# Six U products behind each head's routing, and 70 experts' activations kept ahead of the V loop instead of 42

## The chip, the core and the metric

The kernel runs on one core of a Trainium2 chip. Time is device microseconds (us) of one execution; lower is better. The kernel before takes 3012.7 us, the median of three runs (3009.31 to 3016.61).

## The reference, cut to what matters

Two transformer blocks on 512 tokens of width 1024. The change lies in the last part, `peer_ffn`: every token picks, in each of 8 heads, 16 experts out of 16384 by a product of two key tables, and adds up `gate * gelu(h . u_e) * v_e` over its 128 experts.

```python
s1 = einsum('bshd,hnd->bshn', q[..., :128], keys1)   # 128 scores for each half of the query
s2 = einsum('bshd,hnd->bshn', q[..., 128:], keys2)
v1, i1 = top_k(s1, 16); v2, i2 = top_k(s2, 16)
vals, c = top_k(v1[..., :, None] + v2[..., None, :], 16)
expert = e1 * 128 + e2                               # e1, e2 taken from i1, i2 at c
act = gelu(einsum('td,ted->te', hb, u_tab[eb]))
out = einsum('te,ted->td', gate * act, v_tab[eb])
```

## The kernel before, in words

All fp32 products are made of three matmuls on halves: `load_w` (line 204 on) loads 128x1024 of a weight, ScalarE writes the high part `wh` (line 194), VectorE the rest `wl` (line 195), and `mm3` (lines 200 to 202) multiplies high by high, low by high and high by low. `wraw`, `wh` and `wl` have three buffers each, shared by every weight of the kernel.

`peer` works in this order. First **routing**, eight heads: the query projection (`proj_tr`, tile `acc`, with `yh` and `yl` as the other side), the key scores (line 1550), copies to `q` and `sc` by ScalarE, and in `route` the searches for the top 16 and the sums that turn places into expert numbers, nearly all of it on VectorE. Then **gates**: for 384 tokens (three of the four tiles of 128) the gate of each token and expert is spread into a table of 128 x 128 values, four tokens to a block, 96 blocks: two VectorE instructions (lines 1525 and 1528), 12 small matmuls (1533), one ScalarE copy (1535), and a store to the DRAM table `Gd` for each 16 tokens (1538).

For these 384 tokens all 16384 experts are computed, 128 at a time. `up(e)` makes the **U product** of group e: 24 matmuls of 384 columns into tile `A`, then Gelu into `w`. The **V loop** takes e from 0 to 127: it fetches a piece of the gate table (`g`, eight experts ahead), multiplies `w` by it (line 1471), splits the result into halves, and adds the **V product**, 18 matmuls of 512 columns, to six PSUM banks (`acc`). Two banks are left for `A`.

The first `AHEAD` = 42 U products stand ahead of the V loop. 30 of their results stay in the 31 buffers of `w`; 12 (`SPILL`, every third from 6 to 39) go to DRAM through `wd`, with two buffers `ws`, and are read back in the loop. In an iteration whose e isn't in `SPILL`, the loop makes the next U product.

The last 128 tokens are done by **gathers**, 128 of them, spread over the loop by the table `pace`. One gather (line 1412, GpSimd) reads 128 rows of 8 KB from `uv` by index into `r` (three buffers); VectorE multiplies and adds up (1415), ScalarE does Gelu and the gate (1417, 1418), VectorE adds the result to `x` (1419), which frees the buffer. An iteration's gathers are released by a small ScalarE copy of their indices, `eg` (1486). `pace` gives 9 to an iteration with a U product, 4 to one without that isn't spilled, 0 to a spilled one.

The order on each engine is set by a scheduler when the program is built; the engines then run their instructions strictly in that order.

Of the kernel before, what the change touches and what calls it, by code (L numbers as in the profile page):

```python
# [7 lines left out]
F32 = mybir.dt.float32  # L8
# [4 lines left out]
AF = mybir.ActivationFunctionType  # L13
# [8 lines left out]
LOWP, GDN_AHEAD, SB_AHEAD, U_AHEAD = 1500, 1500, 200, 3000  # L22
# [9 lines left out]

ROT = ((("p", "gd", "p", "sz"), ("g", "gd")), (("p",), ("g",)))

UP = 30
SPILL = range(6, 42, 3)
AHEAD = UP + len(SPILL)


CAND = ((0, 1, 16), (1, 3, 8), (4, 4, 4), (8, 8, 1))  # L40
# [142 lines left out]
class Prog:  # L183
# [664 lines left out]
    def gdn(s, one, two, Y):  # L848
# [14 lines left out]
        for k in range(8):  # L863
            s.mm3(b[:16, :], (wbh[:, 16 * k:16 * k + 16], wbl[:, 16 * k:16 * k + 16]), (Y[0][:, k, :], Y[1][:, k, :]),
                  k == 0, k == 7)
        bf = two.tile([128, NT, 128], F32, name="U", tag="U", bufs=1).rearrange("p t d -> p (t d)")[:16, :]
        nc.vector.tensor_copy(bf, b[:16, :])
# [67 lines left out]
        def head(h):  # L935
# [39 lines left out]

            U, T = BT("U", 1), BT("T", 1)

# [3 lines left out]
            def half(x, m, j):  # L981
                return x.rearrange("p t (b j c) -> p t b j c", j=2, c=m)[:, :, :, j, :]
# [8 lines left out]
            def mh(l, r, m, j, g):  # L991

                r = half(r, m, j)
                o = bank()[:, :128]
                for u, i in enumerate(range(*g)):
                    nc.tensor.matmul(o[:, 64 * u:64 * u + 64], lhsT=l[:, i, :], rhs=r[:, i], start=True, stop=True)
                return o.rearrange("p (t b c) -> p t b c", t=2, c=m)
# [4 lines left out]
            def mm(l, r, g):  # L1002
                o = bank()
                for u, i in enumerate(range(*g)):
                    x = o[:, 128 * u:128 * u + 128]
                    if r is None:
                        nc.tensor.transpose(x, l[:, i, :], s.ident)
                    else:
                        nc.tensor.matmul(x, lhsT=l[:, i, :], rhs=r[:, i, :], start=True, stop=True)
                return o.rearrange("p (t d) -> p t d", t=2)  # L1010
            p1 = part(1)
            for g in pairs:
                w = slice(*g)
                nc.gpsimd.tensor_tensor(U[:, w], s.ident[:, None, :].to_broadcast([128, 2, 128]), p1[:, w], ALU.subtract)
                nc.scalar.activation(T[:, w], mm(U, None, g), AF.Copy)
            for m in LEV:
# [5 lines left out]
                for g in pairs:  # L1022
                    w = slice(*g)
                    u_ = half(U, m, 1)[:, w]
                    nc.vector.tensor_tensor(u_, u_, mh(y, U, m, 1, g), ALU.subtract)
                for g in pairs:
                    w = slice(*g)
                    nc.scalar.activation(half(T, m, 0)[:, w], half(mm(U, None, g), m, 0), AF.Copy)
            A, B = slice(0, 64), slice(64, 128)
            y = two.tile([128, NT, 64], F32, name="y", tag="y", bufs=1)  # L1030
            for g in pairs:
                w = slice(*g)
                o = bank()[:, :128].rearrange("p (t d) -> p t d", t=2)
                for u, i in enumerate(range(*g)):
                    nc.tensor.matmul(o[B, u, :], lhsT=N[A, i, B], rhs=T[A, i, A], start=True, stop=True)
                nc.scalar.activation(y[B, w], o[B], AF.Copy)
            for g in pairs:
                w = slice(*g)
                o = bank()[:, 128:].rearrange("p (t d) -> p t d", t=2)
                for u, i in enumerate(range(*g)):  # L1040
                    nc.tensor.matmul(o[A, u, :], lhsT=y[B, i, :], rhs=U[B, i, B], start=True, stop=True)
                nc.scalar.activation(U[A, w, B], o[A], AF.Copy, scale=-1.0)
            vc, kc = BT("vc", 1), BT("kc", 1)
# [184 lines left out]
    def stick(s, ctx, Y):  # L1228
# [15 lines left out]
        def head(h):  # L1244
# [9 lines left out]
            for js in ((3, 2), (1,), (0,)):  # L1254
# [29 lines left out]
                nc.vector.tensor_tensor(e, e, x[:, :w], ALU.add)  # L1284
                A = two.tile([128, 512], F32, name="A", tag="t1", bufs=1)[:, :w]
                nc.scalar.activation(A, e, AF.Exp)
                for j in js:
# [66 lines left out]
    def peer(s, Y):  # L1354

        nc, tc, a = s.nc, s.tc, s.a
        ND = 128 * DT
        NG = ND // TG
        with ExitStack() as ctx:
            P = lambda name, bufs, **k: ctx.enter_context(tc.tile_pool(reuse_waits="tile", name=name, bufs=bufs, **k))  # L1360
            one, two, gp = P("p_one", 1), P("p_two", 2), P("p_g", 2)
# [7 lines left out]

            s.E = one.tile([128, NT, 2, 128], F32, name="E")  # L1370
            s.gate = one.tile([128, NT, 8, 16], F32, name="gate")
            with tc.tile_pool(reuse_waits="tile", name="p_rt", bufs=2) as rt:
                s.rank = rt.tile([128, 16, 16 * NT], BF, name="rank", bufs=1)
                nc.scalar.activation(s.rank, s.iota[:, :16, None].to_broadcast([128, 16, 16 * NT]), AF.Copy)
                for h in range(8):
                    q = {}

                    def ev(f, b, q=q):
                        q[f] = rt.tile([128, 512], F32, name="q", tag=f"q{f}")
                        nc.scalar.activation(q[f], b, AF.Copy)  # L1380
                    s.proj_tr(Y, a["w_pq"][h], ev, tag="acc", first=h == 0)
                    s.route(rt, q, keys, h)

                g = s.gate.rearrange("p i h r -> p (i h) r")
                n = 8 * NT
                sm = rt.tile([128, n], F32, name="sm")
                nc.vector.tensor_copy(sm, g[:, :, 0])
                nc.vector.tensor_tensor(g, g, sm[:, :, None].to_broadcast([128, n, 16]), ALU.subtract)
                nc.scalar.activation(g, g, AF.Exp)
                nc.vector.tensor_reduce(sm, g, AX.X, ALU.add)  # L1390
                nc.vector.reciprocal(sm, sm)
                nc.vector.tensor_tensor(g, g, sm[:, :, None].to_broadcast([128, n, 16]), ALU.mult)
# [25 lines left out]
                nc.scalar.activation(wt[:, c], wt[:, c], AF.Copy, scale=gx[:, c])  # L1418
                nc.vector.scalar_tensor_tensor(x, r[:, 1024:], wt[:, c], x, op0=ALU.mult, op1=ALU.add)  # L1419
            acc = None  # L1420
            wd = s.dram.tile([len(SPILL), 128, ND], F32, name="wd")

            def up(e):
                with tc.high_priority(offset=U_AHEAD) if e < 6 else nullcontext():
                    U = s.load_w(a["ut"][e], 1024)
                A = s.bank("A")[:, :ND]
                for k in range(8):
                    s.mm3(A, U(128 * k, 128), (Y[0][:, k, :ND], Y[1][:, k, :ND]), k == 0, k == 7)
                if e in SPILL:
                    w = two.tile([128, ND], F32, name="ws", bufs=2)  # L1430
                else:
                    w = two.tile([128, ND], F32, name="w", bufs=UP + 1)
                    wq[e] = w
                nc.scalar.activation(w, A, AF.Gelu)
                if e in SPILL:
                    nc.sync.dma_start(wd[SPILL.index(e)], w)
            wq = {}
            ahead = AHEAD
            for e in range(ahead):
                up(e)  # L1440

            room, n = [0], ahead
            for e in range(128):
                both = e not in SPILL and n < 128
                room.append(room[-1] + (9 if both else 0 if e in SPILL else 4))
# [13 lines left out]
            for e in range(128):  # L1459
                if e not in SPILL and ahead < 128:  # L1460
                    up(ahead)
                    ahead += 1
                if e in SPILL:
                    wq[e] = two.tile([128, ND], F32, name="ws", bufs=2)
                    nc.sync.dma_start(wq[e], wd[SPILL.index(e)])
                if e + 8 < 128:
                    fetch(e + 8)
                w = wq[e]
                w3 = w.rearrange("p (g t) -> p g t", t=TG)
                with tc.issue_after(subs[e - 2].ins) if e > 1 else nullcontext():  # L1470
                    nc.vector.tensor_tensor(w3, w3, gs[e // 8][:, :, e % 8, :], ALU.mult)
                wh = two.tile([128, ND], F32R, name="wh")
                wl = two.tile([128, ND], F32R, name="wl")
                last = s.split(wh, wl, w)
                subs.append(s.sub)
                V = s.load_w(a["uv"][128 * e:128 * e + 128, 1024:], 1024)
                if acc is None:
                    acc = [[s.bank("acc") for n in range(2)] for i in range(DT)]
                for i in range(DT):
                    for n in range(2):  # L1480
                        t = slice(128 * i, 128 * i + 128)
                        s.mm3(acc[i][n], (wh[:, t], wl[:, t]), V(512 * n, 512), e == 0, e == 127)
                js = slice(pace[e], pace[e + 1])
                if js.stop > js.start:
                    with tc.issue_after(last.ins):
                        nc.scalar.activation(eg[:, js], ei[:, js], AF.Copy)  # L1486
                for j in range(js.start, js.stop):
                    gather(j)
# [139 lines left out]
```

## Time and profile before

| | us |
|---|---|
| median of three runs | 3012.7 (3009.31 to 3016.61) |
| the profiled execution | 3021.56 |
| its span | 3019.8 |

| engine | busy us | share of the span |
|---|---|---|
| TensorE matmul (PE) | 2901.3 | 96% |
| TensorE weight load (PEld) | 2602.8 | 86% |
| VectorE (DVE) | 2012.7 | 67% |
| ScalarE (ACT) | 1340.5 | 44% |
| GpSimd (POOL) | 607.4 | 20% |

Busy shares are means over the whole span; matmuls overlap in the trace, so a stretch in which PE is busy all the time can still have few matmuls in it, and their number in a stretch says more. DMA moved 549.62 MB, 182 GB/s over the span; in its last third 277 to 350 GB/s in most stretches of 50 us.

### The profile page before, as it was taken

How to read it: one execution, taken by the hardware profiler on the slowest of the kernel's cores; microseconds unless marked ns; L12 is line 12 of the kernel's file. 1: busy time of each engine (PE TensorE's matmuls, PEld its weight loads, DVE VectorE, ACT ScalarE, POOL GpSimd, SP SyncE). 2: the span in 40 equal slices, each digit the busy share in tenths (PEclk: the TensorE clock that was granted, in tenths of full speed). 3: DMA queues.
4: the chain of work that ended last, by engine and by line, in shares of the span. 5: the costliest groups of instructions: out<-in, count | busy, mean ns of one | idle time of the engine just before them, and what ended most of it. 6: DMA issues, size and time to landing. Idle time of an engine off the chain costs nothing. (4 is left out here: it accounts for less than half of the span.)

```text
span 3019.8 us, 44411 instructions
## 1 busy us (share of the span) xinstructions
PE 2901.3 (96%) x17102; PEld 2602.8 (86%) x17103; DVE 2012.7 (67%) x3633; ACT 1340.5 (44%) x2383; POOL 607.4 (20%) x587
## 2 busy tenths in 40 slices
PE   8999999999899999999999799997999999999998
PEld 7877878888789999999988599997888889988977
DVE  5986445553566676765345997775667788787875
ACT  5244433332455565656423345554334344444432
POOL 3001010000455555452200000000111222222210
PEclk9999999999999999999999899998999999999999
DMA  5321132223345555454763134445788899988985
GB/s 194 98 71 63 57 98 98 97 92 98 109 143 161 150 159 161 137 168 141 228 228 127 53 107 143 169 175 180 244 301 307 297 323 337 334 328 299 332 279 198
DMA packets 200149, 549.62 MB, mean 182 GB/s; under 512 B 17360, under 2 KB 90704, under 8 KB 179072
## 3 DMA queue, kind: packets, MB, share of 16 engines
q1 hardware_dynamic: 149184, 358.34, 36.0%
q0 software_dynamic: 49600, 184.76, 17.5%
q10 hardware_dynamic: 1152, 3.67, 0.4%
q8 instruction: 134, 2.20, 0.3%
q14 instruction: 79, 0.65, 0.1%
HBM read 476.52 MB, written 70.19 MB: 181 GB/s over the span
## 5 line engine op out<-in xcount | busy, mean ns | idle before, releaser
L195 DVE TENSOR_TENSOR wl<-wraw,wh 128x1024 fp32r<-128x1024 f32 x474 | 590.3, 1246 | 305.3 <-ACT wh L194 303.4
L194 ACT ACTIVATE wh<-wraw 128x1024 fp32r<-128x1024 f32 (+1 forms) x495 | 520.8, 1054 | 581.6 <-PE bank L201 126.7
L1412 POOL DMA_INDIRECT r<-in_uv_dram,eg x128 | 175.6, 1372 | 1162.7 <-ACT eg L1486 945.9
L202 PE MATMUL A<-yh,wl 128*128 128x384 f32 x1024 | 346.3, 338 | 7.5 <-DVE wl L195 7.4
L200 PE MATMUL A<-yh,wh 128*128 128x384 f32 x1024 | 345.6, 338 | 3.9 <-ACT wh L194 3.3
L201 PE MATMUL A<-yl,wh 128*128 128x384 f32 x1024 | 344.6, 336 | 0.0
L200 PE MATMUL acc<-wh 128*128 128x512 f32 x768 | 304.1, 399 | 19.4 <-ACT wh L194 19.4
L201 PE MATMUL acc<-wl,wh 128*128 128x512 f32 x768 | 305.5, 398 | 0.9 <-DVE wl L195 0.9
L202 PE MATMUL acc<-wh,wl 128*128 128x512 f32 x768 | 292.6, 397 | 3.8 <-DVE wl L195 3.8
L1415 DVE SCALAR_TENSOR_TENSOR r<-r,hx 128x1024 f32<-128x1024 f32 x128 | 156.3, 1221 | 110.1 <-DMA r<-in_uv_dram,eg 108.7
L200 PE MATMUL p<-yh,wh 128*128 128x256 f32 x736 | 214.1, 291 | 7.0 <-DVE l L195 3.8
L202 PE MATMUL p<-yh,wl 128*128 128x256 f32 x736 | 215.7, 293 | 1.4 <-DVE wl L195 1.4
L201 PE MATMUL p<-yl,wh 128*128 128x256 f32 x736 | 213.4, 290 | 0.0
L202 PEld LDWEIGHTS A<-yh,wl 128*128 128x128 f32 x1024 | 192.9, 188 | 10.6 <-DVE wl L195 10.5
L200 PEld LDWEIGHTS A<-yh,wh 128*128 128x128 f32 x1024 | 193.2, 189 | 8.5 <-ACT wh L194 4.2
L201 PEld LDWEIGHTS A<-yl,wh 128*128 128x128 f32 x1024 | 193.1, 189 | 3.7
L200 PEld LDWEIGHTS acc<-wh 128*128 128x128 f32 x768 | 146.2, 190 | 51.0 <-ACT wh L194 20.8
L201 PE MATMUL bank<-yl,wh 128*128 128x512 f32 (+1 forms) x480 | 184.1, 384 | 0.3 <-DMA yl<-od 0.3
L202 PE MATMUL bank<-yh,wl 128*128 128x512 f32 (+1 forms) x480 | 183.5, 383 | 0.0
L200 PE MATMUL bank<-yh,wh 128*128 128x512 f32 (+1 forms) x480 | 182.8, 383 | 0.1
L202 PEld LDWEIGHTS acc<-wh,wl 128*128 128x128 f32 x768 | 145.2, 189 | 39.0 <-DVE wl L195 5.1
L201 PEld LDWEIGHTS acc<-wl,wh 128*128 128x128 f32 x768 | 146.4, 191 | 33.6 <-DVE wl L195 3.2
(576 smaller groups left out, 6914.8 us busy)
## 6 DMA issues: line engine op xcount, KB each, us to landing
wraw<-in_ut_dram SPq DMA_DIRECT2D x128, 512.0 KB, 4.7
wraw<-in_uv_dram SPq DMA_DIRECT2D x128, 512.0 KB, 6.2
Gd<-g SPq DMA_DIRECT2D x24, 1024.0 KB, 4.4
g<-Gd SPq DMA_DIRECT2D x128, 192.0 KB, 7.6
wraw<-in_w_up_dram SPq DMA_DIRECT2D x44, 512.0 KB, 3.7
wraw<-in_w_sb_dram SPq DMA_DIRECT2D x24, 512.0 KB, 4.3
wraw<-in_w_down_dram SPq DMA_DIRECT2D x22, 512.0 KB, 3.8
wraw<-in_w_out_dram SPq DMA_DIRECT2D x16, 512.0 KB, 3.8
```

What stands on the lines that cost most here:

```text
L194: r = nc.scalar.activation(h, src, AF.Copy)
L195: s.sub = (nc.gpsimd if eng == "pool" else nc.vector).tensor_tensor(l, src, h.bitcast(F32), ALU.subtract)
L200: nc.tensor.matmul(out, lhsT=L[0], rhs=R[0], start=start, stop=False)
L201: nc.tensor.matmul(out, lhsT=L[0], rhs=R[1], start=False, stop=False)
L202: nc.tensor.matmul(out, lhsT=L[1], rhs=R[0], start=False, stop=stop)
L1412: nc.gpsimd.indirect_dma_start(out=r, out_offset=None, in_=a["uv"], in_offset=bass.IndirectOffsetOnAxis(ap=eg[:, j:j + 1], axis=0))
L1415: nc.vector.scalar_tensor_tensor(r[:, :1024], r[:, :1024], 1.0, hx, op0=ALU.mult, op1=ALU.mult, accum_out=act[:, c])
```

## The change

`up`, `wq` and the DRAM tile `wd` are defined ahead of routing, and after each head's `route` six U products follow in the program: 48 of them by the end of routing. `AHEAD` becomes 70, and the other 22 follow after the gates as before. 30 results stay in `w`; the other 40 go through DRAM. `pace` isn't edited, but is worked out from `SPILL` and `AHEAD`, so that it gives nothing to 40 iterations instead of 12 and more to the rest. The V loop makes 58 U products instead of 86.

```diff
-UP = 30
-SPILL = range(6, 42, 3)
-AHEAD = UP + len(SPILL)
+
+AHEAD, UP, UPS = 70, 30, 6
+SPILL = [e for e in range(AHEAD) if e > 1 and e not in {AHEAD * k // (UP - 1) for k in range(UP - 1)}]
...
                     s.proj_tr(Y, a["w_pq"][h], ev, tag="acc", first=h == 0)
                     s.route(rt, q, keys, h)
+                    for e in range(UPS * h, UPS * h + UPS):
+                        up(e)
...
             ahead = AHEAD
-            for e in range(ahead):
+            for e in range(8 * UPS, ahead):
                 up(e)
```

The definition of `up` moves up unchanged, from below the gathers to above the routing:

```python
            def up(e):
                with tc.high_priority(offset=U_AHEAD) if e < 6 else nullcontext():
                    U = s.load_w(a["ut"][e], 1024)
                A = s.bank("A")[:, :ND]
                for k in range(8):
                    s.mm3(A, U(128 * k, 128), (Y[0][:, k, :ND], Y[1][:, k, :ND]), k == 0, k == 7)
                if e in SPILL:
                    w = two.tile([128, ND], F32, name="ws", bufs=2)
                else:
                    w = two.tile([128, ND], F32, name="w", bufs=UP + 1)
                    wq[e] = w
                nc.scalar.activation(w, A, AF.Gelu)
                if e in SPILL:
                    nc.sync.dma_start(wd[SPILL.index(e)], w)
```

The scheduler puts the instructions in another order. Two places show it. The first is ScalarE in routing, from the copies of the scores (`sc`) of one head on; `wh` is the high half of a weight, `q` a projection, `xr` the found places, `w` and `ws` Gelu of a U product. Before (fourth and fifth head):

```order
L1552 ACTIVATE sc<-acc 128x512 x2
L1380 ACTIVATE q<-acc 128x512
L1569 ACTIVATE xr<-ix 128x1024 x2
L194 ACTIVATE wh<-wraw 128x1024
L1380 ACTIVATE q<-acc 128x512
L1552 ACTIVATE sc<-acc 128x512 x2
L194 ACTIVATE wh<-wraw 128x1024
L1380 ACTIVATE q<-acc 128x512
```

Now (sixth head):

```order
L1554 ACTIVATE sc<-acc 128x512 x2
L194 ACTIVATE wh<-wraw 128x1024
L1385 ACTIVATE w<-A 128x384
L194 ACTIVATE wh<-wraw 128x1024
L1385 ACTIVATE ws<-A 128x384
L1571 ACTIVATE xr<-ix 128x1024
L194 ACTIVATE wh<-wraw 128x1024
L1571 ACTIVATE xr<-ix 128x1024
L1385 ACTIVATE w<-A 128x384
L194 ACTIVATE wh<-wraw 128x1024
L1385 ACTIVATE ws<-A 128x384
L194 ACTIVATE wh<-wraw 128x1024
```

Between one head's scores and the next there stood only projections; now six U products stand there, each with its split and its Gelu.

The second place is VectorE at the end of the V loop. `wl<-wraw` is the low half of a V weight, `wl<-w` that of the activations, `w<-w,g` the product with the gates; `r` and `x` belong to the gathers. The last instructions before:

```order
L1471 TENSOR_TENSOR w<-w,g 128x384
L195 TENSOR_TENSOR wl<-wraw,wh 128x1024
L195 TENSOR_TENSOR wl<-w,wh 128x384
L195 TENSOR_TENSOR wl<-wraw,wh 128x1024
L195 TENSOR_TENSOR wl<-w,wh 128x384
L1495 TENSOR_TENSOR r<-r,acc 128x512 x6
```

Now, around the last split; behind the last row here follow six more pairs like the last two rows, and a seventh with the six sums into the output between its two instructions:

```order
L1438 SCALAR_TENSOR_TENSOR x<-r,wt,x 128x1024
L1434 SCALAR_TENSOR_TENSOR r,act<-r,hx 128x1024
L195 TENSOR_TENSOR wl<-w,wh 128x384
L1438 SCALAR_TENSOR_TENSOR x<-r,wt,x 128x1024
L1434 SCALAR_TENSOR_TENSOR r,act<-r,hx 128x1024 x2
L1438 SCALAR_TENSOR_TENSOR x<-r,wt,x 128x1024 x2
L1434 SCALAR_TENSOR_TENSOR r,act<-r,hx 128x1024
L1438 SCALAR_TENSOR_TENSOR x<-r,wt,x 128x1024
```

The last gather stood 8 iterations ahead of the end; now 10 first and 11 second gather instructions stand behind the last split that a V product needs. In all, 45 U products stand ahead of the first V product on TensorE before, and 73 now (the loop's first U products are let in while buffers are free); and of the 96 blocks of gates the last 23 now have no U product beside them, where 8 had none.

## Rows read from the trace of the kernel before

**Rows 1.** Tile acc: count, min/median/max ns, first and last start (us).
```profile
L1533 PE MATMUL acc<-p,ehot x1152: 284/297/303, 1850.0 to 2087.4; 128*128 128x128 bf16 x192
L200 PE MATMUL acc<-wh x768: 387/392/795, 2104.5 to 3013.7; 128*128 128x512 f32 x192
L200 PE MATMUL acc<-yh,wh x144: 278/389/628, 1626.2 to 1754.8; 128*128 128x512 f32 x112, 128*128 128x256 f32 x32
```

**Rows 2.** Timeline of TensorE in the V loop: start, duration, instruction.
```profile
2859.77 0.34 PE L200 MATMUL A<-yh,wh 128*128 128x384 f32 x1
...
2863.96 0.39 PE L200 MATMUL acc<-wh 128*128 128x512 f32 x1
...
2868.14 0.34 PE L200 MATMUL A<-yh,wh 128*128 128x384 f32 x1
```

**Rows 3.** Busy us (instructions) of PE, PEld, DVE, ACT, POOL in routing; then granted clock.
```profile
1700.00:1725.00 25.00, 12.70 (x61) 10.22 (x59) 25.00 (x172) 4.40 (x6) 0.00 (x0) 0.84 0.04 15
1725.00:1750.00 25.00, 19.37 (x85) 16.11 (x85) 25.00 (x140) 6.55 (x8) 0.00 (x0) 0.80 0.23 71
...
1650.00:1825.00 175.00, 150.22 (x771) 135.79 (x771) 174.43 (x990) 68.68 (x89) 0.00 (x0) 0.92 0.28 86
```

**Rows 4.** Timeline of ScalarE in routing: the scores of three heads.
```profile
1712.19 1.22 ACT L1552 ACTIVATE sc<-acc 128x512 f32<-128x512 f32 x2 [1.07 <-issue]
...
1751.52 1.06 ACT L1552 ACTIVATE sc<-acc 128x512 f32<-128x512 f32 x2
...
1762.93 1.08 ACT L1552 ACTIVATE sc<-acc 128x512 f32<-128x512 f32 x2
```

**Rows 5.** Waits of TensorE, 1640 to 1850 us: total, times, longest.
```profile
PE acc L202 <- DVE wl L195: 17.9, 1, 17.9
```

**Rows 6.** VectorE's splits from 1650 to 1825 us, by line: busy, mean ns, idle before.
```profile
L195 DVE TENSOR_TENSOR wl<-wraw,wh 128x1024 fp32r<-128x1024 f32 x27 | 32.5, 1217 | 0.1
```

**Rows 7.** Timeline of the last gate blocks: eight without a U product beside them.
```profile
2073.13 3.56 DVE L1528 TENSOR_TENSOR p<-ehot,T 128x1536 bf16<-128x1536 bf16 x4
...
2076.15 11.50 PE L1533 MATMUL acc<-p,ehot 128*128 128x128 bf16 x96
...
2080.61 0.69 DVE L1525 TENSOR_TENSOR ehot<-iota,T 128x1024 bf16<-128x1024 bf16 x1 [0.41 <-PE acc L1533]
```

**Rows 8.** Waits of TensorE from 2104 to 2300 us.
```profile
PE acc L200 <- ACT wh L194: 16.8, 1, 16.8
```

**Rows 9.** The same view in the V loop; last columns: clock, DMA share, GB/s.
```profile
2872.00:3014.00 142.00, 134.89 (x560) 106.73 (x560) 97.82 (x134) 49.83 (x99) 17.59 (x12) 0.98 0.68 236
2450.00:2800.00 350.00, 346.47 (x1734) 312.41 (x1733) 277.98 (x345) 147.79 (x325) 82.56 (x60) 1.00 0.90 324
```

**Rows 10.** DMA issues: count, KB each, median us from issue to landing.
```profile
wraw<-in_uv_dram SPq DMA_DIRECT2D x128, 512.0 KB, 6.2
g<-Gd SPq DMA_DIRECT2D x128, 192.0 KB, 7.6
...
wd<-ws SPq DMA_DIRECT2D x12, 192.0 KB, 1.9
```

**Rows 11.** Timeline of one gather: issue, first and second VectorE instruction.
```profile
2920.27 1.80 POOL L1412 DMA_INDIRECT r<-in_uv_dram,eg  x1 [10.79 <-DVE wl L195]
...
2928.93 1.23 DVE L1415 SCALAR_TENSOR_TENSOR r<-r,hx 128x1024 f32<-128x1024 f32 x1 [1.18 <-DMA r<-in_uv_dram,eg]
...
2932.15 1.28 DVE L1419 SCALAR_TENSOR_TENSOR x<-r,wt,x 128x1024 f32<-128x1024 f32 x1
```

**Rows 12.** VectorE's gather instructions in the loop, by line: busy, mean ns, idle before.
```profile
L1419 DVE SCALAR_TENSOR_TENSOR x<-r,wt,x 128x1024 f32<-128x1024 f32 x128 | 163.7, 1279 | 12.8 <-ACT wt L1418 12.8
L1415 DVE SCALAR_TENSOR_TENSOR r<-r,hx 128x1024 f32<-128x1024 f32 x128 | 156.3, 1221 | 110.1 <-DMA r<-in_uv_dram,eg 108.7 <-DMA g<-Gd 0.9
```

**Rows 13.** Waits from 2130 to 2990 us: GpSimd.
```profile
POOL r L1412 <- ACT eg L1486: 945.9, 70, 505.9
```

**Rows 14.** Timeline of the end: the last split of activations, and the stores.
```profile
3006.63 0.56 DVE L195 TENSOR_TENSOR wl<-w,wh 128x384 fp32r<-128x384 f32 x1 [2.00 <-ACT wh L194]
3013.38 2.72 SPq L1498 DMA_DIRECT2D out_dram<-r  x3
```

More of the change, by code (lines that the diff above doesn't have):

```diff
@@ L1371, in peer, with up @@
             s.gate = one.tile([128, NT, 8, 16], F32, name="gate")
+            wd = s.dram.tile([len(SPILL), 128, ND], F32, name="wd")
+            def up(e):
+                with tc.high_priority(offset=U_AHEAD) if e < 6 else nullcontext():
+                    U = s.load_w(a["ut"][e], 1024)
+                A = s.bank("A")[:, :ND]
+                for k in range(8):
+                    s.mm3(A, U(128 * k, 128), (Y[0][:, k, :ND], Y[1][:, k, :ND]), k == 0, k == 7)
+                if e in SPILL:
+                    w = two.tile([128, ND], F32, name="ws", bufs=2)
+                else:
+                    w = two.tile([128, ND], F32, name="w", bufs=UP + 1)
+                    wq[e] = w
+                nc.scalar.activation(w, A, AF.Gelu)
+                if e in SPILL:
+                    nc.sync.dma_start(wd[SPILL.index(e)], w)
+            wq = {}
             with tc.tile_pool(reuse_waits="tile", name="p_rt", bufs=2) as rt:
@@ L1420, in peer @@
             acc = None
[L1421 to L1437, printed above, removed]
             ahead = AHEAD
-            for e in range(ahead):
+            for e in range(8 * UPS, ahead):
                 up(e)
```

## The prediction

> **What bounds the kernel now.** I read the stages first, from the first and last start of the matmuls into `acc` [rows 1]: routing's projections from 1626.2 us, gates from 1850.0 to 2087.4, V products from 2104.5 to 3013.7. The reader is to see three stretches: 224 us of routing with the first U products, 238 us of gates, and 909 us of V loop.
>
> Then the timeline of TensorE in the loop [rows 2]: a U product starts at 2859.77, the next V product at 2863.96, the next U product at 2868.14. So a U product costs 4.19 us and a V product 4.18 us of TensorE, back to back. The order gives 45 U products ahead of the loop, hence 83 + 128 = 211 products in it: 882 us of its 909. The loop is TensorE-bound, with some 27 us lost. In it VectorE is busy 277.98 of 350 us, and DMA moves 324 GB/s at a share of 0.90 [rows 9]: both are second bounds not far away.
>
> Last the stretches of routing [rows 3]: VectorE is busy all the time, TensorE issues 61 and 85 matmuls in 25 us at a granted clock of 0.84 and 0.80. One pair of heads shows the hole: the scores of one head come at 1712.19, of the next at 1751.52, and then at 1762.93 [rows 4], 39.3 us against 11.4. TensorE waits 17.9 us there for one weight split [rows 5], which in VectorE's order stands behind the routing of two heads; the slow clock does the rest.
>
> **The change part by part.**
>
> *Products moved.* 73 instead of 45 U products stand ahead of the loop: 28 x 4.19 = 117 us more there, 117 less in the loop. Net 0: moving work on a full engine gains nothing, only filled holes do.
>
> *The hole in routing.* With U products behind each head it should close: 39.3 - 11.4 = **-28**. A head then costs TensorE 11.4 + 6 x 4.19 = 36.5 us. VectorE needs for it (174.4 - 32.5) / 8 = 18 us of routing [rows 3, 6], as nearly all eight heads lie in that stretch, and 8 splits of 1.22 us (six U, two projection): 28 us. So VectorE keeps up. Its order has three splits ahead of each head's searches and the fourth behind 27 short instructions, about 6 us, while three products feed TensorE for 12.5. ScalarE, busy 68.7 of 175 us [rows 3], has room for 48 splits and Gelus. For handovers at the projection's end I add **+4** (0 to +10). The gain's ends: -34, if slack at the other heads goes too, and -5, if splits still wait behind routing.
>
> *Gates.* The last 23 blocks instead of 8 have no U product beside them. Eight take TensorE 11.5 us, 1.44 each; VectorE needs 3.56 / 4 + 0.69 = 1.58 a block [rows 7]. 15 x 0.14 = **+2**. The wait for the gate table through DRAM, 16.8 us [rows 8], stays: no U product is left for it, as before.
>
> *Spills.* 28 more stores and reads of 192 KB on SP's queue. Each store waits there for its Gelu, with the next weight loads behind it; but three weight buffers are 12.5 us of products, a load lands in 6.2 and such a store in 1.9 [rows 10]. **0**; without that cover at most 28 x 1.9 = +53, which I exclude, since a store's wait ends with its own product.
>
> *The loop, denser.* The 128 gathers and 128 V weights must now pass in fewer products. In VectorE's order 47 gathers stand from e = 72 to 104, beside 32 V and 28 U products: 60 loads of 0.524 MB, 32 gate pieces of 0.197, 47 gathers of 1.05 make 87 MB in 60 x 4.18 = 251 us, 347 GB/s. From 104 to 128 it is 36 MB in 100 us. DMA has held 324 GB/s for 350 us at a share of 0.90 [rows 9]; in proportion a full share is 360. So it just fits: **+6**, between 0 and, if 324 were the limit, 123 MB / 324 = 379 us instead of 351, +28. VectorE fits too: 47 x (1.22 + 1.28) + 60 x 1.22 + 64 x 0.55 = 226 of 251 us [rows 6, 12, 14]. The 27 us lost elsewhere in the loop I leave; they could shrink by some 15.
>
> *The end.* This is the term that decides. Before, the gathers ran on ScalarE's release, not on buffers: GpSimd waited 945.9 us for `eg` [rows 13], and the last gather lay 8 iterations ahead of the end. Now `pace` gives nothing to 40 iterations, so the gathers start late and then come at the pace of their three buffers; in VectorE's fixed order 10 first and 11 second instructions stand behind the last split. Nothing can put them earlier. Lower end: 10 x 1.22 + 11 x 1.28 = 26.3 us [rows 12], and 7 for sums and store, against 3019.8 - 3006.6 = 13.2 from the last split to the end now [rows 14]: +20. Upper end: at the cycle of a buffer inside the loop, issue at 2920.27, second instruction done at 2933.4 [rows 11], 13.2 / 3 = 4.4 a gather: 44 + 7 - 13 = +38. With the weight loads gone the 8.7 us from issue to landing must shorten, so I take the middle, 3.4 a gather: **+28**.
>
> What a lone gather would take is not in this trace. The Trainium skill's page "DMA: Bandwidth & Descriptors" (Anatomy of one DMA — SWDGE (gpsimd) path) gives a fit of 2.0 us plus bytes over 436 GB/s, an estimate of 4.4 us for 1.05 MB, half of the 8.7 seen under load. By it a buffer's cycle would be 4.4 + 4.5 = 8.9 us, 3.0 a gather, the end +24 instead of +28 and the sum lower by 4.
>
> **Sum:** -28 + 4 + 2 + 0 + 6 + 28 = **+12 us**. The profiled execution took 3021.56 (span 3019.8 and 1.8 around it), 8.9 above the median of 3012.7; it becomes 3034, and the median **3025**.
>
> **Rivals.**
> *Faster.* The loop sheds its own waits: with 55 U products in it instead of 83, fewer loads share the three weight buffers, and of the 27 us lost 14 go; the gathers at the end run at VectorE's floor and DMA costs nothing: -28 + 2 + 20 - 14 = -20, **2993**. It decides once the loop's losses fall below some 20 us with the end at its floor. Against it: 12 of the 27 are lost in the last 142 us, which hold 31 V products worth 130 and hardly a U product [rows 9], and there the gathers now get denser.
> *No change.* End at the floor, DMA free: -28 + 4 + 2 + 20 = -2, **3011**.
> *DMA-bound.* The dense part runs at 324 GB/s and late gathers stop VectorE, as 108.7 us of waits for them do already [rows 12]; the end runs at 4.4 a gather: -28 + 4 + 2 + 28 + 38 = +44, **3057**.
> *The change doesn't do what it says.* TensorE still waits for splits in routing, -5 instead of -28: +35, **3048**.
>
> **How the numbers follow.** About 0.2% (6 us) is what a measurement can tell from no change. Forecast, +6 to +25: 0.35. DMA-bound: 0.22. Routing not filled: 0.10. No change: 0.15. Faster: 0.18. So faster 0.18, same 0.15, slower 0.67. The range, 2996 to 3056, leaves out the outer halves of the faster and of the DMA-bound case, 0.2 in all. The slower cases alone reach from 3019 to 3060.
>
> **What would show it.** Right: no stretch of routing with under 100 matmuls in 25 us; first V product 117 - 28 + 4 + 2 = 95 us later, near 2200; last V product 909 - 117 + 6 = 798 us behind it, near 2998; then 20 to 40 us in which only VectorE, ScalarE and gathers work, with GpSimd waiting for `x` instead of `eg`. Wrong: holes left in routing; a loop with far fewer than 250 matmuls in 50 us; or gathers that are done when the last V product ends. If the loop lasts under 780 us on TensorE, the faster rival is true; if over 815, the DMA-bound one.

## The result, and the profile after

The changed kernel takes 3038.7 us (median of five runs, 3028.9 to 3043.5), the kernel before 3009.9 beside it (3008.6 to 3016.6): a ratio of 1.0081, 95% interval 1.0060 to 1.0102, so 18 to 31 us slower. The forecast was slower, 3025 with a range of 2996 to 3056. The profiled execution took 3038.29 us with a span of 3036.5.

In the code of the changed kernel the gather stands in line 1431, VectorE's two instructions for it in 1434 and 1438, the copy `eg` in 1488, the gate matmuls in 1535. First tile `acc` again, with the columns of [rows 1]:

```profile
L1535 PE MATMUL acc<-p,ehot x1152: 285/298/303, 1949.9 to 2169.6; 128*128 128x128 bf16 x192
...
L200 PE MATMUL acc<-wh x768: 388/393/793, 2184.5 to 2993.4; 128*128 128x512 f32 x192
...
L202 PE MATMUL acc<-wh,wl x768: 387/393/628, 2189.4 to 2995.0; 128*128 128x512 f32 x192
L200 PE MATMUL acc<-yh,wh x144: 283/389/562, 1623.3 to 1899.4; 128*128 128x512 f32 x112, 128*128 128x256 f32 x32
```

The first V product starts at 2184.5 instead of 2104.5, and the V loop lasts 810.5 us instead of 909.7. Against [rows 1] the span divides like this:

| | before | after | products moved | what is left |
|---|---|---|---|---|
| first V product at | 2104.5 | 2184.5 | 28 x 4.19 = +117 | -37 |
| V loop (first to last start of its V matmuls) | 909.7 | 810.5 | -117 | +18 |
| last V product to the span's end | 5.6 | 41.5 | | +36 |
| span | 3019.8 | 3036.5 | | +17 |

The last matmul of the loop stands on line 202, before at 3014.2, after at 2995.0. The two profiled executions differ by 17 us, the medians by 29. The profiled run of before lay 9 to 12 us above its medians, that of after at its own, so 12 us of the difference are in no trace: no run shows in which stretch a faster execution of before saves them.

Routing and the loop by windows; columns as in [rows 3], the last two being the DMA share and GB/s:

```profile
1700.00:1725.00 25.00, 25.00 (x138) 23.24 (x137) 16.15 (x65) 8.50 (x12) 0.00 (x0) 1.00 0.39 122
1725.00:1750.00 25.00, 25.00 (x131) 23.07 (x130) 19.73 (x87) 10.18 (x13) 0.00 (x0) 1.00 0.48 142
1650.00:1825.00 175.00, 175.00 (x958) 165.35 (x957) 135.35 (x618) 68.67 (x93) 0.00 (x0) 1.00 0.43 133
...
2300.00:2750.00 450.00, 430.31 (x2017) 370.23 (x2016) 337.60 (x430) 176.74 (x371) 106.31 (x66) 0.99 0.89 312
2750.00:2900.00 150.00, 150.00 (x725) 131.74 (x724) 123.78 (x158) 63.22 (x144) 37.02 (x26) 1.00 0.93 335
2900.00:3000.00 100.00, 88.35 (x364) 69.71 (x362) 86.05 (x114) 38.68 (x87) 30.68 (x19) 0.95 0.84 299
3000.00:3036.00 36.00, 0.00 (x0) 0.00 (x0) 20.97 (x27) 3.49 (x14) 6.93 (x5) 0.50 0.80 293
```

The hole in routing is gone: TensorE is busy 175.00 of 175 us with 958 matmuls at a granted clock of 1.00 (the 2.4 GHz level), against 150.22, 771 and 0.92, a mixture of the two levels, before [rows 3]. From 2300 to 2750 the loop has become thin: 430.31 of 450 us and 2017 matmuls, where the kernel before had, in the same window,

```profile
2300.00:2750.00 450.00, 446.81 (x2228) 401.63 (x2226) 353.49 (x440) 189.36 (x414) 102.62 (x75) 1.00 0.90 324
```

Part of the smaller number is the mix: a V product has 18 matmuls, a U product 24, and both take about 4.2 us. In the last 36 us TensorE does nothing at all.

TensorE's only wait from 1640 to 2200 us worth naming, in the list of waits (total, times, longest), stands where that of [rows 8] stood:

```profile
PE acc L200 <- ACT wh L194: 14.6, 1, 14.6
```

Who waits in the loop, in the same list from 2200 to 2960 us:

```profile
POOL r L1431 <- ACT eg L1488: 897.9, 28, 596.2
POOL r L1431 <- DVE x L1438: 245.2, 58, 13.2
...
ACT wh L194 <- PE acc L201: 102.0, 60, 3.5
DVE r L1434 <- DMA r<-in_uv_dram,eg: 97.8, 44, 8.9
```

GpSimd now also waits for buffers (`x`, 245.2 us), and VectorE 97.8 us for gathers that haven't landed; in the kernel before that was 93.8 us in the same window. The timeline of the end, from the last split of activations:

```profile
2987.48 0.55 DVE L195 TENSOR_TENSOR wl<-w,wh 128x384 fp32r<-128x384 f32 x1
...
2989.37 1.22 DVE L1434 SCALAR_TENSOR_TENSOR r<-r,hx 128x1024 f32<-128x1024 f32 x1
...
2995.62 1.94 POOL L1431 DMA_INDIRECT r<-in_uv_dram,eg  x1 [4.22 <-DVE x L1438]
...
3002.28 1.23 DVE L1434 SCALAR_TENSOR_TENSOR r<-r,hx 128x1024 f32<-128x1024 f32 x1 [2.50 <-DMA r<-in_uv_dram,eg]
...
3021.86 1.23 DVE L1434 SCALAR_TENSOR_TENSOR r<-r,hx 128x1024 f32<-128x1024 f32 x1 [0.77 <-DMA r<-in_uv_dram,eg]
...
3024.97 1.28 DVE L1438 SCALAR_TENSOR_TENSOR x<-r,wt,x 128x1024 f32<-128x1024 f32 x1
...
3026.27 0.32 SPq L1494 DMA_DIRECT2D r<-x  x1
...
3031.06 1.28 DVE L1497 TENSOR_TENSOR r<-r,acc 128x512 f32<-128x512 f32 x2 [3.62 <-DMA r<-x]
```

Ten gathers are used behind that split, from 2989.37 to 3021.86: nine steps of 3.61 us. The last ends at 3026.25, and 10.2 us of sums and stores follow: the sums' inputs `r<-x` use the gathers' buffers, so the last of them is loaded only at 3026.27, and VectorE waits 3.62 us for it.

### The profile page after: what moved, and what is told of

It reads as the page before. It is cut to its first block, busy times and chain, and to the rows that moved or that the text cites. A ratio compares the mean times of both kernels' runs of the same rounds, so it can differ in the third digit from the quotient of the medians.

```text
span 3036.5 us, 44530 instructions
## 1 busy us (share of the span) xinstructions
PE 2899.4 (95%) x17103; PEld 2599.8 (86%) x17103; DVE 2018.9 (66%) x3633; ACT 1341.6 (44%) x2364; POOL 631.7 (21%) x587
## 4 chain that ended last, share of the span: by engine, by line
PE 68%; DMA 10%; issue 10%; DVE 7%; POOL 3%; ACT 2%; SPq 0%; DVEq 0%; POOLq 0%; ACTq 0%
PE bank L201 6%; PE bank L200 6%; PE bank L202 6%; DMA r<-in_uv_dram,eg 5%; PE A L202 4%; PE A L200 4%; PE A L201 4%; PE acc L1535 4%; PE p L200 4%; PE p L201 3%; PE p L202 3%; PE acc L201 3%; PE acc L200 3%; PE acc L202 3%; PE gd L996 2%
## 5 line engine op out<-in xcount | busy, mean ns | idle before, releaser
L1431 POOL DMA_INDIRECT r<-in_uv_dram,eg x128 | 198.8, 1553 | 1197.6 <-ACT eg L1488 897.9
L200 PE MATMUL acc<-wh 128*128 128x512 f32 x768 | 280.0, 400 | 22.4 <-ACT wh L194 22.4
L202 PE MATMUL acc<-wh,wl 128*128 128x512 f32 x768 | 286.1, 397 | 0.5 <-DVE wl L195 0.5
```

The lines of the kernel that those rows point to most:

```text
L200: nc.tensor.matmul(out, lhsT=L[0], rhs=R[0], start=start, stop=False)
L202: nc.tensor.matmul(out, lhsT=L[1], rhs=R[0], start=False, stop=stop)
L1431: nc.gpsimd.indirect_dma_start(out=r, out_offset=None, in_=a["uv"], in_offset=bass.IndirectOffsetOnAxis(ap=eg[:, j:j + 1], axis=0))
```

## The experiments

**What is the filled hole worth alone?** Two kernels go back to 42 experts ahead, 12 of them through DRAM, and keep products behind each head: five in one, as shown, and three (`42, 30, 3`) in the other.

```diff
-AHEAD, UP, UPS = 70, 30, 6
-SPILL = [e for e in range(AHEAD) if ...]
+AHEAD, UP, UPS = 42, 30, 5
+SPILL = range(6, 42, 3)
```

Five: 

> The V loop, the spills and the pace as in the kernel before (42 ahead, 12 through DRAM), but 40 of the 42 U products behind the heads' routing, five each, so that none is left for the gates. Theory: the hole in routing closes (about -37 us, as in the changed kernel's first V product), but the 96 gate blocks run without U products at VectorE's 1.58 us instead of TensorE's 1.37, which gives back 96 x 0.2 = 20 us: about 3010 - 17 = 2993. Rival (gates alone run at TensorE's pace): about 3010 - 37 = 2973.

Three: 

> The V loop, the spills and the pace as in the kernel before, 24 of the 42 U products behind the heads' routing, three each, 18 left for the gates. Theory: the hole in routing closes and the gates keep enough U products to stay on TensorE, the loop and its end are those of before: first V product near 2104 - 35 = 2069, time about 3010 - 35 = 2975 us. Rival (the gain of the changed kernel ahead of the loop came from having more U products there, not from filling the hole): less than 10 us faster than before, above 3000.

Measured: 2985.8 us, ratio to before 0.9895 [0.9868, 0.9922], and 2983.4 us, 0.9893 [0.9873, 0.9913]. Tile `acc` of the kernel with three, and one window of its gates:

```profile
L1535 PE MATMUL acc<-p,ehot x1152: 282/297/302, 1865.2 to 2056.6; 128*128 128x128 bf16 x192
L200 PE MATMUL acc<-wh x768: 387/392/792, 2072.2 to 2984.5; 128*128 128x512 f32 x192
```
```profile
2000.00:2050.00 50.00, 49.79 (x413) 46.22 (x414) 50.00 (x69) 37.47 (x35) 0.00 (x0) 1.00 0.46 190
```

As many products stand ahead of the loop as before, and the first V product comes 32.3 us earlier; the loop lasts 912.7 us as against 909.6. The filled hole is worth 32 us, and 24 products fill it as well as 40 or 48. With three behind each head the theory came out; with five the time lies between the theory's 2993 and the rival's 2973. The rest of the change, from 42 to 70 experts ahead, costs 3038.7 - 2983.4 = 55 us, or 60 with each kernel taken against the kernel before that ran beside it. The window shows that gate blocks without a U product pass at 413 / 12 = 34.4 in 50 us, 1.45 us each, with VectorE and TensorE both full.

**More experts ahead, the hole left as it was.**

```diff
-AHEAD, UP, UPS = 70, 30, 6
+AHEAD, UP, UPS = 70, 30, 0
```

> UPS from 6 to 0 in the changed kernel: 70 activations ahead of the V loop as before, but all behind routing, none behind a head. Theory (the gain of the change is the filled hole alone, about 37 us, and everything else in it is loss): the first V product comes at 2104.5 + 25 x 4.19 = about 2209 us, the loop and the end stay as in the changed kernel (some 815 + 41), so the span ends near 3066, 30 us or more behind the changed kernel. Rival (the U products between the heads cost VectorE and ScalarE elsewhere what they fill): the first V product at about 2185 to 2195 and a span like the changed kernel's, 3036.

Measured: two runs, 3044.5 and 3064.1 us, ratio 1.0130 [1.0085, 1.0175]. The interval overlaps that of the changed kernel, so it isn't shown to be slower than that, and the spans of the profiled executions differ by only 6 us (3042.7 and 3036.5). The first V product starts at 2190.8, 18 us ahead of the theory's 2209, in the range that the rival had named, but not for its reason: routing has its hole as before, and what is gone is the wait of [rows 8]. TensorE's waits from 1640 to 2200 us:

```profile
PE acc L202 <- DVE wl L195: 17.9, 1, 17.9
...
PE acc L1552 <- ACT q L1397: 4.0, 1, 4.0
```
```profile
2093.00:2191.00 98.00, 98.00 (x567) 97.97 (x566) 30.63 (x28) 35.34 (x51) 0.00 (x0) 1.00 0.62 199
```

The window between the last gate block and the first V product is full of U products: they ran while the gate table came back through DRAM. Products put behind routing's heads fill one hole and are no longer there for the other. Both holes need only a few, as the next kernel shows.

**Four products held back for the second hole.** On the kernel with three products behind each head, the 42nd to the 45th U product are kept on TensorE behind the last gate matmul (`s.glast`).

```diff
-            def up(e):
+            def up(e, after=None):
...
-                for k in range(8):
-                    s.mm3(A, U(128 * k, 128), ...)
+                with tc.issue_after(after) if after else nullcontext():
+                    for k in range(8):
+                        s.mm3(A, U(128 * k, 128), ...)
...
-                up(e)
+                up(e, s.glast.ins if e >= ahead - 1 else None)
...
-                    up(ahead)
+                    up(ahead, s.glast.ins if ahead < AHEAD + 3 else None)
```

> The kernel with 42 activations ahead and three products behind each head, with four U products (the 42nd to the 45th) held on TensorE behind the last gate block, so that they run while the gate table comes back from DRAM. In that kernel TensorE waited 15.3 us for the first V product there, and with none behind routing the 23 products behind the gates had hidden this wait. Theory: 4 x 4.19 = 16.8 us of products cover the 15.3, all before moves up by as much, and the time falls from 2983 by 12 to 15 us, to about 2970. Rival (the gates' stretch had hidden those four products already, so that they only come later): 2983.

Measured: 2971.8 us, 0.9847 [0.9828, 0.9866]: as the theory said, and 1.5% better than before, the fastest kernel here that still makes the whole result. The first V product comes at 2060.3, 11.9 us earlier than with three products and none held. Its longest wait of TensorE from 1640 to 2090 us:

```profile
PE A L200 <- ACT wh L194: 1.0, 1, 1.0
```

**Still fewer ahead.** The same with 33 experts ahead, three through DRAM (`AHEAD, UP, UPS = 33, 30, 3`, `SPILL = range(6, 33, 12)`).

> As the kernel with four held products, with 33 activations ahead in place of 42, three of them through DRAM: nine more U products in the loop. Theory (the loop loses to gathers what they crowd, so a longer loop loses less): of the 17 us that the loop loses with 42 ahead some 5 go, with the hold a time of about 2965. Rival (ahead or not is a zero sum, and what the loop loses doesn't depend on nine products): the same as with 42, 2970.

Measured: 2984.3 us, 0.9897 [0.9880, 0.9914], a miss for both. The loop lasts 950.9 us for 93 + 128 products worth 924, so it loses 27 us; with 42 ahead and the hold it lost 899.9 - 882 = 18, in the other traces with 42 ahead 25 to 31. VectorE's wait for gathers is 155.4 us here against 111.3. More U products in the loop didn't make it lose less. VectorE's order differs too: 95 of the 128 gathers are used ahead of the split of the iteration after theirs, where 53 were with 42 ahead.

**The end: an even pace.** The changed kernel with gathers also in the iterations whose expert was spilled:

```diff
-                room.append(room[-1] + (9 if both else 0 if e in SPILL else 4))
+                room.append(room[-1] + (9 if both else 4))
```

> The change, with 4 instead of 0 in the table that paces the gathers for an iteration whose activations come from DRAM, so that gathers also run in those 40 iterations. Nothing else differs. In VectorE's order all 128 gathers now stand ahead of the last split. Theory (the gathers start too late and run on behind the loop): the end shrinks from 41 us behind the last V product to about 8, the loop stays near 811 us, time about 3038.7 - 32 = 3007 us. Rival (the loop is bound by DMA bytes, the gathers only move): the loop grows by what the end loses, from 811 to about 840 us, time 3030 or more.

Measured: 3018.2 us, 1.0001 [0.9986, 1.0016], between theory and rival. The last gather is done at 2987.6, ahead of the last V product at 3019.4, and the 36 us of the end are gone; but the loop grew from 811 to 831 us in an execution 9 us above this kernel's median. Waits of GpSimd, ScalarE and VectorE in it, from 2200 to 2960 us:

```profile
POOL r L1431 <- DVE x L1438: 400.8, 89, 14.4
ACT wh L194 <- PE acc L201: 175.3, 87, 3.6
DVE wl L195 <- ACT wh L194: 139.1, 95, 7.8
```

**What do the gathers cost the loop?** The changed kernel without gathers:

```diff
-                    with tc.issue_after(last.ins):
-                        nc.scalar.activation(eg[:, js], ei[:, js], AF.Copy)
-                for j in range(js.start, js.stop):
-                    gather(j)
```

> The change without its gathers: the experts' sum of the last 128 tokens is left out. Theory (the loop's 46 us beyond its products are waits of VectorE, ScalarE and the loads on the gathers): the loop falls from 811 to 183 x 4.18 = 765 plus at most 15, and nothing follows it: about 2184 + 780 + 6 = 2970 us. Rival (they are weight loads and splits that come late by themselves): the loop stays above 800, time near 2995.

Measured: one run, 2965.6 us. The loop lasts 767.6 us for 183 products, worth 765. All but 3 us of what the dense loop loses, it loses to the gathers. The next five kernels ask to what in them.

**Half the bytes; narrow instructions; a fourth buffer.**

Three kernels, each the changed one with a single edit. Half the bytes:

```diff
-                nc.gpsimd.indirect_dma_start(out=r, out_offset=None, in_=a["uv"],
+                nc.gpsimd.indirect_dma_start(out=r[:, :1024], out_offset=None, in_=a["uv"].rearrange("e (b c) -> (e b) c", b=2),
...
-                nc.vector.scalar_tensor_tensor(x, r[:, 1024:], wt[:, c], x, op0=ALU.mult, op1=ALU.add)
+                nc.vector.scalar_tensor_tensor(x, r[:, :1024], wt[:, c], x, op0=ALU.mult, op1=ALU.add)
```

Narrow instructions:

```diff
-                nc.vector.scalar_tensor_tensor(r[:, :1024], r[:, :1024], 1.0, hx,
+                nc.vector.scalar_tensor_tensor(r[:, :256], r[:, :256], 1.0, hx[:, :256],
...
-                nc.vector.scalar_tensor_tensor(x, r[:, 1024:], wt[:, c], x, op0=ALU.mult, op1=ALU.add)
+                nc.vector.scalar_tensor_tensor(x[:, :256], r[:, 1024:1280], wt[:, c], x[:, :256], op0=ALU.mult, op1=ALU.add)
```

Four buffers, for which two of the activations kept in `w` make room (42 then go through DRAM instead of 40):

```diff
-AHEAD, UP, UPS = 70, 30, 6
+AHEAD, UP, UPS = 70, 28, 6
...
-            rows = P("p_rows", 3)
+            rows = P("p_rows", 4)
```

What was expected:


Half: 

> Each gather of the changed kernel moves 4 KB a row instead of 8 KB, and both VectorE instructions read that half: the number of instructions, their lengths and the three buffers stay, 67 MB of transfers go. The rows gathered are other ones, so the last 128 tokens' expert sum comes out as other numbers. In the instructions' order all gathers now stand ahead of the last split, as in the kernel with an even pace, whose loop lasted 831 us. Theory (the bytes limit the dense loop): the loop falls to 770 to 795 us. Rival (the three buffers' cycle or VectorE's order limits it, not the bytes): 815 to 831 us.

Narrow: 

> The two VectorE instructions of each gather work on 256 columns instead of 1024; gathers move all their bytes. The last 128 tokens' expert sum is thereby left incomplete. Takes some 128 x 1.9 = 240 us of work off VectorE, and shortens the cycle of a buffer by about 2 us. All gathers stand ahead of the last split here too. Theory (bytes): the loop stays at 815 to 831 us. Rival (VectorE's share of the cycle, or splits that stand behind waiting gather instructions): 770 to 795 us.

Four: 

> Four buffers for gathered rows instead of three; to make room UP goes from 30 to 28, so 43 activations go through DRAM instead of 41 or so. All gathers stand ahead of the last split. Theory (bytes limit the dense loop): as with the even pace, the loop lasts about 831 us, there is no tail, and the time is near that kernel's 3018. Rival (the cycle of three buffers limits it: issue, 9 us of landing, two VectorE instructions): a fourth buffer gives each gather a third more time, the loop falls to about 795, the tail stays away, and the time is 2980 to 2990.

Measured, beside the even pace:

| | loop, us | DMA share, 2700 to 2800 | VectorE busy there | VectorE's wait for gathers | time, us | ratio |
|---|---|---|---|---|---|---|
| even pace | 831.3 | 0.89 | 76.6% | 9.9 | 3018.2 | 1.0001 [0.9986, 1.0016] |
| half the bytes | 828.7 | 0.72 | 84.3% | 167.3 | 3018.5 | 1.0017 [0.9998, 1.0035] |
| narrow | 822.9 | 0.90 | 50.7% | 131.8 | 3009.2 | 0.9986 [0.9971, 1.0001] |
| four buffers | 830.2 | 0.92 | 84.0% | 59.5 | 3029.1 | 1.0059 [1.0037, 1.0080] |

Loop, shares and waits are those of the profiled executions, which lay 9, 1 and 10 us above their kernels' medians and 6 below, in the table's order; so differences of 10 us between these loops say nothing. All four have their gathers done ahead of the loop's end, and all four loops last 823 to 831 us, far above 795. Half the bytes, less work on VectorE or a fourth buffer alone don't free the loop: with half the bytes the DMA share drops to 0.72 and the loop stays.

That doesn't clear the bytes altogether, for each edit also gave VectorE another order. With half the bytes 43 of the 128 gathers are used ahead of the split of the iteration after theirs, with an even pace one, with narrow instructions none and with four buffers two. And ScalarE waits for weights that haven't landed (`ACT wh <- DMA wraw`, 2200 to 3000 us) 72, 71 and 95 us in the three kernels with full bytes, 41 us with half of them.

**Both at once.** Half the bytes and narrow instructions together:

> Both at once on the changed kernel: gathers of 4 KB a row, and VectorE's two instructions for each on 256 columns; the last 128 tokens' expert sum comes out as other numbers. With half the bytes alone the loop lasted 828.3 us, with narrow instructions alone 822.6, without gathers 767.2. Theory now (two bounds of about the same height, DMA and VectorE: taking one away leaves the other): with both gone the loop falls to 770 to 790 us. Rival (neither is it: what counts is that a gather's instruction on VectorE waits for its data with the next split behind it, as often with small gathers as with large): the loop stays at 810 or more.

Measured: 3012.6 us, 0.9985 [0.9973, 0.9998], a loop of 819.0 us: the rival's side. VectorE is busy half of the time, DMA has a quarter free, and 54 us are lost. Waits from 2200 to 2985 us, and two windows:

```profile
POOL r L1431 <- ACT eg L1488: 1101.5, 66, 597.1
DVE r L1434 <- DMA r<-in_uv_dram,eg: 307.4, 111, 7.4
POOL r L1431 <- DVE x L1438: 50.1, 7, 8.6
```
```profile
2200.00:2600.00 400.00, 397.43 (x1872) 342.29 (x1871) 218.98 (x387) 162.91 (x322) 74.21 (x55) 1.00 0.75 244
2600.00:2900.00 300.00, 272.18 (x1259) 234.01 (x1259) 153.52 (x306) 114.27 (x273) 69.51 (x58) 0.97 0.71 232
```

Counted by products, 46 of the 54 us are lost from e = 72 to 104 (2618.8 to 2903.4), where most iterations have a U and a V product and release two gathers. The timeline of VectorE, GpSimd and TensorE in one such iteration shows how:

```profile
2699.99 0.56 DVE L195 TENSOR_TENSOR wl<-w,wh 128x384 fp32r<-128x384 f32 x1
2700.31 1.04 POOL L1431 DMA_INDIRECT r<-in_uv_dram,eg  x1 [7.87 <-ACT eg L1488]
...
2701.66 1.41 POOL L1431 DMA_INDIRECT r<-in_uv_dram,eg  x1 [0.30 <-issue]
...
2704.53 0.42 DVE L1434 SCALAR_TENSOR_TENSOR r<-r,hx 128x256 f32<-128x256 f32 x1 [2.27 <-DMA r<-in_uv_dram,eg]
...
2709.85 0.42 DVE L1434 SCALAR_TENSOR_TENSOR r<-r,hx 128x256 f32<-128x256 f32 x1 [3.76 <-DMA r<-in_uv_dram,eg]
...
2711.30 0.56 DVE L195 TENSOR_TENSOR wl<-w,wh 128x384 fp32r<-128x384 f32 x1
2711.63 1.05 POOL L1431 DMA_INDIRECT r<-in_uv_dram,eg  x1 [8.56 <-ACT eg L1488]
...
2713.62 0.44 PE L202 MATMUL A<-yh,wl 128*128 128x384 f32 x1 [0.64 <-DVE wl L195]
```

It is a ring. The gathers of an iteration are released by `eg`, which stands on ScalarE behind the split of that iteration's activations; VectorE's instructions for them stand ahead of the next iteration's split. So a turn takes issue, landing and use of the iteration's last gather: from 2699.99 to 2711.30 it is 11.3 us, where its two products need 8.4. In this kernel 96 of the 128 gathers are used like that, ahead of the next split; in the changed kernel none is.

**The ring cut.** The same kernel with each gather's instructions behind the split two iterations on, and six half-width buffers in the space of three:

```diff
+            acc, pend = None, [[], []]
...
                 subs.append(s.sub)
+                with tc.issue_after(s.sub.ins):
+                    for p in pend.pop(0):
+                        finish(*p)
+                pend.append([])
...
-                    gather(j)
+                    pend[-1].append(gather(j))
```

> The kernel with gathers of 4 KB a row and narrow VectorE instructions, with six buffers of half the width in place of three, and VectorE's two instructions for a gather put behind the split of the activations two iterations after the one that issues it, instead of about one. The last 128 tokens' expert sum comes out as other numbers. With bytes halved and VectorE half idle the loop still lasted 819 us, and VectorE waited 307.4 us in 111 waits for gathers still on their way. Theory (each such wait keeps the splits behind it on VectorE, and with them TensorE): a gather gets some 4.2 us more, VectorE's wait for gathers falls below 100 us, and the loop falls to 770 to 785 us. Rival (the loop loses to something else that gathers do, GpSimd's issues or the transfers' share of the queues): the wait falls too, but the loop stays at 805 or more.

Measured: two runs, median 2959.7 us, 0.9831 [0.9790, 0.9872]; the loop lasts 767.2 us, as without gathers. VectorE's gather instructions by line, as in [rows 12], and a window, in this kernel:

```profile
L1437 DVE SCALAR_TENSOR_TENSOR r<-r,hx 128x256 f32<-128x256 f32 x128 | 49.6, 419 | 1.1 <-DMA r<-in_uv_dram,eg 1.1
```
```profile
2700.00:2800.00 100.00, 100.00 (x504) 90.63 (x503) 59.64 (x120) 45.94 (x108) 35.39 (x24) 1.00 0.85 282
```

VectorE's wait falls from 307.4 to 1.1 us, and TensorE is full. With the same bytes and the same work, the later use and the three further buffers that it takes gave back 52 us. Six buffers in the old order weren't tried; that they would have done little is argued from the waits above, where GpSimd waited 50.1 us for buffers and, after the first gather, 504 us for `eg`. Whether later use helps gathers of 8 KB a row wasn't tried either: four such buffers already took the room of two activations, and at the full bytes the DMA share was 0.89 to 0.92. The kernel with an even pace lost 66 us though VectorE waited only 9.9 us for data; there GpSimd waited 400.8 us for buffers, ScalarE and VectorE for one another, and which of these carries its loss stays open.

## Why the prediction was right, point by point

The sign, the range and the shape were right: the filled hole is worth less than what the thinner loop and the end cost. Three terms of the sum were sized too small, one of them for a reason that the runs don't bear out. That the sum came close is partly luck: the gain ahead of the loop was 15 us larger than its terms, the loop and the end together 20 us dearer, and the two nearly cancel, +12 forecast and +17 in the traces. The other 12 us of the 29 between the medians are the profiled execution of before, which lay high; I took 9 us off for the changed kernel as well, and its profiled execution lay at its median.

*Products moved*, 0: as said. With +117 ahead of the loop and -117 in it the table above adds up to the span's +17.

*The hole in routing*, -28 with handovers of +4, and *Gates*, +2: together -22, measured -37 at the first V product. With as many products ahead as before it was -32. No handover is to be seen: 175.00 of 175 us busy at a clock of 1.00, where I had taken one slow pair of heads and left the slack at the other heads for the range's end (-34). The gates' +2 wasn't there: a block without a U product takes 1.45 us, not VectorE's sum of 1.58, next to the 1.44 of [rows 7]. That the wait for the gate table stays was right (14.6 us), and I took it as given; four held products later gave back 12 us of it.

*Spills*, 0: right. With 40 of them VectorE waits 2.8 us for spilled activations, and a kernel without gathers but with all spills loses 2.6 us in its loop.

*The loop, denser*, +6 with ends of 0 and +28: measured +18 in the trace, from 27 to 46 us lost. The step that failed is its reason. I weighed bytes against the bandwidth alone (347 GB/s wanted, 360 to be had, for the stretch from e = 72 on). In that stretch the forecast held: from the V product of e = 72 at 2637.1 to that of e = 104 at 2883.8 pass 247 us for 57 products, 8 us lost, where the kernel before lost 7, and TensorE is full from 2750 to 2900 at 335 GB/s. Nearly all of the 18 us were lost where I had left the sum as it was: ahead of e = 72, where most iterations now have a V product alone, the loss grew from 10 to 26 us; behind e = 104 it went from 10 to 11. What I had in hand was 108.7 us of VectorE's waits for gathers [rows 12], and I read them as a sign of full DMA. The runs with light gathers show that such waits can come from the order, with bytes to spare.

Which of the two makes the 46 us with full gathers stays open. It isn't the ring as shown, for none of the changed kernel's gathers is used ahead of the next split. 57 are used ahead of the split after that, and before these stand 96 of the 104 us that VectorE waits for gathers from the loop's start to the span's end; 93 of them lie ahead of 2640, where the loss grew. A ring of two turns would look like this, for two turns of a V product alone are 8.4 us and half of the gathers here take over 8.7 us to land; so would transfers that land late for want of bandwidth: ScalarE, too, waits 69 us for weights in this loop, against 4 us in the kernel with the ring cut.

*The end*, +28 (+20 to +38): measured +36, from 13.2 to 49.0 us behind the last split. The count of 10 and 11 instructions was right. A gather took 3.61 us instead of 3.4, and sums and stores 10.2 instead of 7, because the residual loads share the gathers' buffers. This was the right place to look: with an even pace the end is gone, but 20 of its 36 us come back in the loop by the traces, and some 12 by the ratios of the two kernels to before.

At 2995.62 a gather of 1.05 MB was issued, and VectorE had it at 3002.28, 6.7 us later, with others in flight, while DMA moved 293 to 299 GB/s at a share of 0.80 to 0.84. In the ring's timeline one of 0.52 MB, issued at 2700.31, was first used at 2704.53, after 4.2 us. One gather of the changed kernel flew alone: issued at 2932.64, the one before it landed at 2931.07 and no other queue moved a packet until it had landed itself, after 5.6 us. By the fit on the Trainium skill's page "DMA: Bandwidth & Descriptors" (Anatomy of one DMA — SWDGE (gpsimd) path), 2.0 us plus bytes over 436 GB/s, the estimates are 4.4 us for 1.05 MB and 3.2 us for 0.52 MB. The measurements decide: they are 1.0 to 2.3 us longer, and 1.2 us longer for the gather that flew alone.

Of the rivals, *DMA-bound* named a loop of over 815 us and 4.4 us a gather; it came to 811 and 3.61, between it and the forecast. *Faster* needed a loop under 780 us; here only light gathers used later, or no gathers, gave that.

## What to carry to other kernels

Moving work on a full engine pays only by the holes it fills: find each hole, give it as many products as it holds (24 behind the heads, four behind the gates), and leave the rest where other work needs its cover. Look for rings through a loop's in-order engines: a transfer released by one iteration and used ahead of the next one's split sets a floor to the turn (11.3 us here for 8.4 us of products, with light gathers) that neither bandwidth nor engine time shows. An edit that changes a transfer also lets the scheduler change the order, so look at the order again before the edit is taken for a test of the transfer. A table that spreads work over iterations has to be looked at again when a constant that feeds it changes.

## What the runs showed of the hardware that I had not expected

Two relieved resources at once can leave a loop as slow as it was: 54 us lost with DMA at a share of 0.71 to 0.75 in the stretches from 2200 to 2900 us and VectorE busy half of the time, and 2 us with the same bytes and work in another order and six buffers instead of three. A gather of 1.05 MB that had all queues to itself took 5.6 us from issue to landing. And in gate blocks VectorE's two instructions, of 0.69 and 3.56 us (the latter for four) [rows 7], pass at 1.45 us a block, below their sum of 1.58, with VectorE shown busy all the time: a sum of durations from a timeline can be some 9% too high.
